# State-space B loaded in its final layout, and C turned with full 128x128 transposes, in a two-layer hybrid backbone step

## The chip, the cores and the metric

The kernel is one program on one NeuronCore of a Trainium2 chip. The time is device microseconds of one launch, the median of several runs. The engines are named as in the profile: PE is the matrix engine (PEld its weight loads), DVE the vector engine, ACT the scalar engine, POOL the general engine, SP the engine that issues most DMAs.

## What is computed

The reference is one inference step of a backbone with two layers over 128 context tokens and 512 latent tokens, 1024 channels wide. A layer normalises and shifts x, projects it once, runs three branches (a gated DeltaNet with scans in both directions, a diagonal complex state-space layer called S5, and a pooling mixer), adds the gated branches through an output projection and ends with a convolutional feed-forward network (FFN). What matters here is S5's input and output matrices: 32 groups, 64 complex states each, 16 channels.

```
bb_re = f_re[..., None] * b_re - f_im[..., None] * b_im      # b (G, P, 16), f (G, P)
bb_im = f_re[..., None] * b_im + f_im[..., None] * b_re
bu_re = einsum("blgc,gpc->blgp", u, bb_re)                   # u (B, L, G, 16)
x = scan of bu with the powers of lambda, once per direction
y = einsum("blgp,gcp->blgc", x_re, c_re) - einsum("blgp,gcp->blgc", x_im, c_im)
```

In DRAM `ssm_b_*[l]` is (32 groups, 64 states, 16 channels) and `ssm_c_*[l]` is (32 groups, 16 channels, 64 states), in float32.

## The kernel before

All activations lie channel-major: a tile is 128 channels by 640 tokens (512 latent, 128 context). A projection (`mm3`, lines 377 to 389) multiplies a 128-column tile of weights with eight such tiles; weights and activations are split into two float32r parts each, and three products per pair are added, so a tile of 1024 rows is 48 matmuls of 320 columns. The weights of a tile come by one 512 KB DMA on SP's queue (`wraw`, line 359, four buffers, shared with the modulation's weights `wada`, line 443), ACT makes the upper part (`whi`, line 371) and DVE the lower part (`wlo`, line 372), each in two halves with four buffers.

The S5 branch of a layer (`s5_chain`) is a chain of dependent steps: u is projected, sent to DRAM and read back in another order by eight SP loads (line 1044); `s5_params` makes the tables; `s5_in` (lines 909 to 930) turns the table of each quad of groups with four 128x128 transposes per part (line 915) and multiplies (line 920); `s5_scan` runs the recurrence on DVE; `s5_out` makes y. A `Weave` fills the chain's gaps: wherever the chain yields a number of microseconds, pieces of independent work (projections of the z gates, pools, branch gates, q and k, and parts of the modulation at line 446) are emitted for as long. Within these orders a scheduler with a simulated timeline sets the order of each engine's instructions; each engine then runs its own in order, and waits in order. SBUF space comes from an arena that hands out columns; a tile waits until the last users of its columns are done.

`s5_load` issues the parameter loads on POOL's queue: the rates and states (line 713), the step sizes (line 716), then B and C, real and imaginary, each as 32 rows (one per group) of 1024 values (lines 717 to 719). For layer 0 it is emitted at the start; for layer 1 it is one of the pieces that hang on the tiles of layer 0's FFN, with `s5_params` four pieces later, shortly before the last two tiles of the FFN and the next norm (`turn`, with its DVE lines 572 and 581).

`s5_params` first transposes the rates (line 735), has ACT and DVE make exponentials, sines and the powers of lambda (lines 749 to 829), and brings B and C to the layout [(direction, state), (group, channel)], 128 partitions by 512 columns: for each of the four tensors and each of the 16 channels a transpose of a [32 groups, 64 states] block (line 841) gives the upper 64 partitions of a PSUM bank and a product with the identity (line 842) the same in the lower 64, and ACT moves the bank to SBUF in the order of channels (line 845). Then DVE multiplies B with f (lines 862 to 867) and the skip weights are turned (line 876). The copies of ACT through PSUM carry line 235 in the profile, since a helper records them.

Of the kernel before, what the change touches and what calls it, by code (L numbers as in the profile page):

```python
# [17 lines left out]
P = 128  # L18
# [11 lines left out]
G = 32  # L30
# [10 lines left out]
WK, WB = 4, 4               # blocks of a split weight tile, and how many tiles stand  # L41
# [4 lines left out]
# columns of the constant table  # L46
C_ID, C_D16, C_TF, C_TB, C_BD = 0, 128, 144, 272, 400  # C_D16: row c' of a 32-row block against column c
C_M = 528                       # masks of the levels: the halves of 32 against each other, of 64; of a
                                # triangle in every second block, the other one in those between: 16, 32, 64
C_HALF = C_M + 5 * 128          # first and second half of 32  # L50
C_I16 = C_HALF + 2
C_EDGE = C_I16 + 16             # 4 windows x (8 left, 8 right)
C_POSR = C_EDGE + 64            # 4 tiles x 8 rows
C_POSC = C_POSR + 32            # 4 tiles x 64 columns
# [3 lines left out]
def constants():  # L58
# [26 lines left out]
    for n, w in enumerate(POOL_WINDOWS):  # L85
        h = w // 2
        for t in range(h):
            c[:, C_EDGE + 16 * n + t] = np.float32(w) / np.float32(t + h)
        for t in range(h - 1):          # t-th of the last h-1 positions
            c[:, C_EDGE + 16 * n + 8 + t] = np.float32(w) / np.float32(w - 1 - t)  # L90
# [4 lines left out]
class Arena:  # L95
    """SBUF in pages of some columns. A page holds data of one type at a time: a tile that stands while
    any of its columns is taken. Columns are handed out in program order, those free longest first,
    and next to blocks of the same size."""

    def __init__(self, pool, pages):  # L100
        self.pool = pool
        self.pages = [Page(i, n) for i, n in enumerate(pages)]
        self.clock = self.made = 0
        self.keep = True                # the largest page is kept free
        self.side = False               # of the work being emitted: a chain of steps, or what fills its gaps

    def take(self, cols, dt=F32, stays=False, most=None, big=False):
# [3 lines left out]
        for pg in self.pages:  # L111
# [3 lines left out]
            for s in pg.gaps(k):  # L115
# [4 lines left out]
                if stays:               # what stays long fills the pages already begun  # L120
                    key = (key[0], far, odd, not pg.blocks, key[-1])
# [18 lines left out]
class Page:  # L140
# [5 lines left out]
    def gaps(self, k):  # L146
        """Starts of the free places of k units: at either end of a gap, and every k units."""
        at = 0
        for b, e in self.blocks + [(self.n, self.n)]:
            if b - at >= k:  # L150
                yield from range(at, b - k + 1, k)
                yield b - k
            at = e
# [11 lines left out]
class Part:  # L165
    """Some columns of a Buf; the last part to go frees it."""
# [10 lines left out]
class Blocks:  # L177
    """Tiles of up to WK blocks, one after the other."""
# [10 lines left out]
class Weave:  # L189
    """Emits a chain of dependent steps with pieces of independent work in between: the chain yields  # L190
    how long (us of TensorE) it would leave the engine idle at a point."""
# [7 lines left out]
    def add(self, cost, fn, weights=None):  # L199
        """weights: prepares what fn takes, one piece of work ahead."""  # L200
# [23 lines left out]
class ScalarE:  # L224
    """The engine; remembers its last instructions that want another table set than that of Ln and Exp."""
# [15 lines left out]
def together(*gens):  # L241
    """Steps of several chains in turn."""
# [17 lines left out]
def hybrid_dit_kernel(ctx: ExitStack, tc: tile.TileContext, a, outs, depth=DEPTH, taps=None):  # L260
# [47 lines left out]
    def hv(ap):  # L308
        """[P, NT] as two halves."""
        return ap.rearrange("p (h n) -> p h n", h=2)  # L310

    # ------------------------------------------------------------------ parameters
    def rows_load(name, rows, E):
        """rows: list of (dram rows [r, 128], first row)."""
# [5 lines left out]
    def to_cols(name, rt, n):  # L320
        """The first n rows as columns [P, n]."""
# [9 lines left out]
    def load_params(l, E):  # L331
        fc = a["ffn_conv"][l].rearrange("t (r c) -> t r c", c=P)
        o = 0 if l else -56                                    # layer 0's b_ada and norm1_g come with glob
# [21 lines left out]
    # ------------------------------------------------------------------ weights  # L355
    def wraw(src, c0, nk, ncols):
        """Weight rows of src (nk*128, .) columns c0.. as [P, nk, ncols]."""
# [4 lines left out]
    def wsplit(raw, m):  # L362
        """128 columns of a raw block as two float32r parts whose sum is the block."""
# [13 lines left out]
    def mm3(ps, w, hs, first=True, last=True, M=P):  # L377
        """ps[M, 2, HF] (+)= w^T h with the products hi*hi, hi*lo and lo*hi."""
# [12 lines left out]
    def mm3k(ps, w, k, h_, first, last):  # L391
        """The part of mm3 of one tile of h; ps: the two halves."""
# [7 lines left out]
    def mmh(ps, w, k, h_, h, first, last):  # L400
        """The part of mm3 of one tile of h, one half."""
# [5 lines left out]
    def split(src, hi, lo, scale=None):  # L407
        """src [P, n] float32 (times scale, a power of two) -> float32r parts."""
# [13 lines left out]
    class Stream:  # L422
        """m-tiles of a weight matrix."""
# [7 lines left out]
    # ------------------------------------------------------------------ adaLN  # L431
    def ada_pieces(l, p, mod, grp, E=None):
        """Columns grp*2048.. of the modulation into mod [P, 2, 48], in pieces."""
# [18 lines left out]
        def finish():  # L452
# [5 lines left out]
            # column (j, b) of the group is m-tile grp*16 + 4*j + b  # L458
# [8 lines left out]
    # ------------------------------------------------------------------ norms  # L467
    @contextmanager
    def ln_exp():
        """ScalarE's table set that has both Ln and Exp, for what is emitted inside."""  # L470
# [8 lines left out]
    def rsq(ps2, n, scale, dst, bias=None):  # L479
        """dst = (scale*ps + eps)^-1/2 * e^bias over [P, NT] in two halves."""  # L480
# [9 lines left out]
    def square_sum(tot, x, i):  # L490
        """tot += x^2"""
# [8 lines left out]
    def spans(cut):  # L500
        """Columns and stream of the parts before and after a cut of the latents."""
        return ((0, cut, 0),), ((cut, LAT, 0), (CX, NT, 1))

    def last_tiles(xs, ws, hs, gate, cut, tot, sq, between, done):
        """The last two tiles (weights ws) of a projection onto x, all of them up to the cut first; between(): when
        the first is through; done(h): after each part. tot: the squares of the tiles before, then also of the last
        but one; sq: of the last."""
# [29 lines left out]
    def turn(xs, ws, hs, gate, tot, A, B, raws):  # L537
        """The last two tiles of a projection onto x, h = x / rms(x) * A + B per stream (A, B [P, 2, 8]; tot: the
        squares of the tiles before), and the first products of the next two weight tiles, as h comes; also an
        instruction that what follows on VectorE should queue behind."""  # L540
# [87 lines left out]
    def finale(xs, xg, ws, hs, gate, tot):  # L628
        """The last two tiles of the last projection, the norm, token-major again; xg: the tiles before times
        the norm's weights."""  # L630
# [43 lines left out]
    def scales(mod, c0, g):  # L674
        """(1 + scale) * g per stream."""
# [13 lines left out]
    def residual(x, ps, gate, i):  # L689
        """x += gate * ps per stream; gate [P, 2, 8]."""  # L690
# [6 lines left out]
    def conv3(y, r, w0, w2):  # L697
        """y (= w1*u) += w0*u[t-1] + w2*u[t+1] inside each stream."""
# [4 lines left out]
    # ------------------------------------------------------------------ S5  # L703
# [3 lines left out]
    def s5_load(l, E, kept):  # L707
# [9 lines left out]
        for nm in ("ssm_b_re", "ssm_b_im", "ssm_c_re", "ssm_c_im"):  # L717
            ld[nm] = ar.take(SP * GC)
            E.dma_start(ld[nm].f[:G, :], a[nm][l].rearrange("g x y -> g (x y)"))
# [8 lines left out]
    def s5_params(ld):  # L728
        """Discretisation; tables over [(dir, p), g]."""
# [23 lines left out]
        # sin and cos: ang - 2 pi round(ang / 2 pi), the multiple taken off in parts  # L753
# [14 lines left out]
        # cos(r) = sin(pi/2 - |r|)  # L768
# [4 lines left out]
        # powers 0..9 of lb over [ri, power, g]  # L773
# [7 lines left out]
        def cmul(dst, x, y, n):  # L781
            """dst[:, ri, n] = x * y (complex, all [P, 2, n, G])."""
# [11 lines left out]
        # f = (lb - 1) / lam  # L794
# [15 lines left out]
        # tables in the order each half (direction) wants: H = 0 forward, 1 backward  # L810
        cp = small("s5_cp", 2 * 10 * G)                        # C side: forward 0..9, backward 9..0
        q["cp"] = cp.rearrange("p (r j g) -> p r j g", r=2, j=10)
        bp = small("s5_bp", 2 * 8 * G)                         # B side: forward 7..0, backward 0..7
# [7 lines left out]
        # step of the recurrence over [ri, g]: lb^8 and its imaginary part signed  # L821
# [9 lines left out]
        # b and c transposed to [(dir, p), (g, channel)]  # L831
        tr = {}
        W = G * GC + GC
        kept, temp = ld["kept"], ar.take(3 * W)
        for nm in ("ssm_b_re", "ssm_b_im", "ssm_c_re", "ssm_c_im"):
            raw = ld[nm]
            ps = sm()
            for c in range(GC):
                src = (raw.f[:G].rearrange("g (p c) -> g c p", c=GC)[:, c] if "_b_" in nm
                       else raw.f[:G, c * SP:(c + 1) * SP])  # L840
                PE.transpose(ps[0:SP, c * G:(c + 1) * G], src, ident[:G, :G])
                PE.matmul(ps[SP:P, c * G:(c + 1) * G], src, ident[:G, :G], start=True, stop=True,
                          tile_position=(0, SP))
            t = Part((kept if "_c_" in nm else temp).f[:, W * (nm[-1] == "m"):][:, :W])
            S.activation(t.f[:, :G * GC].rearrange("p (g c) -> p c g", c=GC),
                         ps.rearrange("p (c g) -> p c g", c=GC), AF.Copy)
            raw.free()
            tr[nm] = t
        q["cre"], q["cim"] = tr["ssm_c_re"], tr["ssm_c_im"]
        bre, bim = tr["ssm_b_re"], tr["ssm_b_im"]  # L850
# [8 lines left out]
        t0 = Part(temp.f[:, 2 * W:2 * W + G * GC])  # L859
# [8 lines left out]
        temp.free()  # L868
# [1270 lines left out]
```

## Time and profile before

| | |
|---|---|
| median of three runs | 2631.55 us (2629.29 to 2636.67) |
| span of the profiled execution | 2633.5 us (of its time only the span is listed) |
| PE busy | 2501.0 us, 95% |
| DVE, ACT, POOL busy | 1592.6, 996.0, 543.3 us |
| mean granted TensorE clock | 0.966 |
| DMA | 296.29 MB, mean 113 GB/s |

The busy time of an engine is the time in which it runs an instruction. Engines run beside each other, so shares don't add up. The granted clock is the share of TensorE's full speed that the chip gave it: 1.00 is 2.4 GHz, 0.50 is 1.2 GHz. A wait is put down to the instruction whose end released it.

### The profile page before, as it was taken

The numbers are of one execution on the slowest core, as the hardware profiler recorded it, in microseconds if no ns is written. First come the engines' busy times: TensorE is split into PE (matmuls) and PEld (weight loads), VectorE is DVE, ScalarE is ACT, GpSimd is POOL, SyncE is SP. The second block draws the span as 40 slices with busy tenths as digits, with TensorE's granted clock in tenths as the row PEclk, the third lists the DMA queues.
The fourth block names the chain that finished last, engine by engine and source line by source line (L and its number), as shares of the span: only waits on it lengthen the run. The fifth ranks groups of instructions, "written<-read, shape, count | busy, mean of one in ns | idle before, by whom it ended". The sixth has DMA issues, their size and how long they took to land. (4 is left out here: it accounts for less than half of the span.)

```text
span 2633.5 us, 44415 instructions
## 1 busy us (share of the span) xinstructions
PE 2501.0 (95%) x17593; PEld 2366.6 (90%) x17593; DVE 1592.6 (60%) x3250; ACT 996.0 (38%) x1796; POOL 543.3 (21%) x552
## 2 busy tenths in 40 slices
PE   8989999998899999999988989999988999999998
PEld 6868988998899989999977979979888999999998
DVE  5467874269785543644565587733797866445355
ACT  4233343354234432433333423423532445334243
POOL 2241150134451000000123213301345420000000
PEclk9799999999899999999978989999999999999999
DMA  9642327434352355222227223374434422222221
GB/s 302 99 133 84 112 74 230 119 123 134 119 164 88 107 177 168 77 76 73 76 73 99 56 73 106 88 220 112 135 131 139 154 73 73 73 80 74 73 73 65
DMA packets 381635, 296.29 MB, mean 113 GB/s; under 512 B 33578, under 2 KB 336372, under 8 KB 381428
## 3 DMA queue, kind: packets, MB, share of 16 engines
q1 hardware_dynamic: 377892, 286.53, 38.0%
q0 software_dynamic: 3168, 6.68, 1.0%
q8 instruction: 139, 2.28, 0.4%
q14 instruction: 68, 0.56, 0.1%
q10 hardware_dynamic: 368, 0.25, 0.0%
HBM read 250.92 MB, written 42.48 MB: 111 GB/s over the span
## 5 line engine op out<-in xcount | busy, mean ns | idle before, releaser
L384 PE MATMUL acc<-pg,whi 128*128 128x320 f32 x4064 | 948.5, 314 | 7.6 <-ACT pg L235 5.5
L386 PE MATMUL acc<-pg,whi 128*128 128x320 f32 x4064 | 942.5, 312 | 3.1 <-DVE pg L411 3.0
L388 PE MATMUL acc<-pg,wlo 128*128 128x320 f32 x4064 | 936.4, 311 | 9.4 <-DVE wlo L372 9.4
L384 PEld LDWEIGHTS acc<-pg,whi 128*128 128x128 f32 x4064 | 683.3, 190 | 47.6 <-issue 22.3
L372 DVE TENSOR_TENSOR wlo<-wraw,whi 128x512 fp32r<-128x512 f32 (+1 forms) x538 | 406.2, 761 | 524.8 <-ACT whi L235 516.2
L388 PEld LDWEIGHTS acc<-pg,wlo 128*128 128x128 f32 x4064 | 686.4, 190 | 13.3 <-DVE wlo L372 9.6
L386 PEld LDWEIGHTS acc<-pg,whi 128*128 128x128 f32 x4064 | 687.4, 190 | 8.5 <-DVE pg L411 4.1
L235 ACT ACTIVATE whi<-wraw 128x512 fp32r<-128x512 f32 (+1 forms) x538 | 331.8, 623 | 926.9 <-PE acc L386 708.5
L235 ACT ACTIVATE pg<-pg 128x640 f32<-128x640 f32 (+8 forms) x335 | 223.3, 682 | 254.6 <-DVE pg L1993 56.6
L235 ACT ACTIVATE pg<-sm 128x512 f32<-128x512 f32 (+12 forms) x249 | 115.6, 486 | 274.3 <-PE sm L915 64.7
L235 ACT ACTIVATE pg<-acc 128x640 f32<-128x640 f32 (+3 forms) x196 | 126.7, 654 | 52.5 <-PE acc L388 35.2
L411 DVE TENSOR_TENSOR pg<-pg,pg 128x640 fp32r<-128x640 f32 x84 | 70.6, 847 | 41.1 <-ACT pg L235 36.0
L700 DVE SCALAR_TENSOR_TENSOR pg<-pg,cols_f 128x511 f32<-128x511 f32 x126 | 63.8, 548 | 42.3 <-ACT pg L235 42.2
L713 POOL DMA_DIRECT2D pg<-in_ssm_lambda_re_dram x2 | 1.2, 578 | 408.2 <-DVE pg L732 408.2
L691 DVE SCALAR_TENSOR_TENSOR pg<-acc,mod,pg 128x320 f32<-128x320 f32 x56 | 30.8, 550 | 77.1 <-PE acc L388 77.0
L1682 POOL TENSOR_TENSOR pg<-pg,pg 128x640 f32<-128x640 f32 x21 | 40.2, 1915 | 175.0 <-DVE pg L1680 110.8
L235 ACT ACTIVATE pg<-acc,cols_f 128x640 f32<-128x640 f32 (+1 forms) x88 | 68.3, 776 | 0.0
L1680 DVE SCALAR_TENSOR_TENSOR pg<-pg,acc 128x640 f32<-128x640 f32 x48 | 39.2, 816 | 42.8 <-PE acc L388 39.1
L701 DVE SCALAR_TENSOR_TENSOR pg<-pg,cols_h 128x511 f32<-128x511 f32 x126 | 63.5, 546 | 0.0
L569 POOL TENSOR_SCALAR pg<-pg,ada_a 128x320 f32<-128x320 f32 (+2 forms) x27 | 26.5, 990 | 158.1 <-DVE pg L691 102.9
L446 PE MATMUL sm<-wada,silu_c 128*32 128x512 f32 x320 | 55.2, 604 | 0.8 <-DMA wada<-in_w_ada_dram 0.8
L903 POOL TENSOR_TENSOR pg<-pg,pg 128x512 f32<-128x512 f32 (+1 forms) x32 | 53.8, 1684 | 1.6
(397 smaller groups left out, 3065.8 us busy)
## 6 DMA issues: line engine op xcount, KB each, us to landing
wraw<-in_w_in_dram SPq DMA_DIRECT2D x96, 512.0 KB, 4.4
wraw<-in_ffn_w_up_dram SPq DMA_DIRECT2D x88, 512.0 KB, 3.9
wada<-in_w_ada_dram SPq DMA_DIRECT2D x80, 512.0 KB, 4.5
wraw<-in_ffn_w_down_dram SPq DMA_DIRECT2D x32, 512.0 KB, 3.7
mg_dram<-pg SPq DMA_DIRECT2D x32, 320.0 KB, 2.2
pg<-mg_dram SPq DMA_DIRECT2D x32, 320.0 KB, 4.7
wraw<-in_w_out_dram SPq DMA_DIRECT2D x16, 512.0 KB, 3.8
pg<-in_w_ada_dram SPq DMA_DIRECT2D x6, 1024.0 KB, 12.1
```

The source lines that it names most:

```text
L235: ins = self.engine.activation(out, in_, func, **kw)
L372: V.tensor_sub(lo, src, hi)
L384: PE.matmul(ps[:M, h, :HF], hi[:, k, :M], hh[:, h * HF:(h + 1) * HF], start=first and k == 0, stop=False)
L386: PE.matmul(ps[:M, h, :HF], hi[:, k, :M], hl[:, h * HF:(h + 1) * HF], start=False, stop=False)
L388: PE.matmul(ps[:M, h, :HF], lo[:, k, :M], hh[:, h * HF:(h + 1) * HF], start=False, stop=last and k == n - 1)
L411: V.tensor_sub(lo.r, src, hi.r)
L446: PE.matmul(ps[q:q + 32, :], silu_c[:, k, :], t[:, j * 512:(j + 1) * 512], start=k == 0, stop=k == KT - 1, tile_position=(0, q))
L700: V.scalar_tensor_tensor(y[:, b + 1:e], r[:, b:e - 1], w0, y[:, b + 1:e], op0=OP.mult, op1=OP.add)
L701: V.scalar_tensor_tensor(y[:, b:e - 1], r[:, b + 1:e], w2, y[:, b:e - 1], op0=OP.mult, op1=OP.add)
L903: E.tensor_tensor(oo, oo, t.f, op=OP.add if r else OP.subtract)
L1680: V.scalar_tensor_tensor(hv(g_.f), hv(g_.f), 1.0, ps[:, :, :HF], op0=OP.add, op1=OP.mult)
L1682: GP.tensor_tensor(g_.f, g_.f, mg.f, op=OP.add)
```

## The change

`s5_load` now loads B straight into the layout in which it is used, into the first 64 partitions, in runs of 16 channels, and copies these to the other 64 partitions by a DMA that reads SBUF. C is loaded with (group, channel) on the partitions, four blocks of 128 rows side by side, and each row twice, once for each direction. In `s5_params` B needs no array operation any more; C is turned by four transposes of a [128, 128] block for the real and four for the imaginary part, and ACT moves each bank as it stands. The scratch tile of the products with f has its own space. All comments and docstrings of the file are dropped too, line by line, so that line numbers move little.

```
@@ s5_load @@
-        for nm in ("ssm_b_re", "ssm_b_im", "ssm_c_re", "ssm_c_im"):
-            ld[nm] = ar.take(SP * GC)
-            E.dma_start(ld[nm].f[:G, :], a[nm][l].rearrange("g x y -> g (x y)"))
+        with nc.allow_non_contiguous_dma(reason="runs of 16 channels"):
+            for nm in ("ssm_b_re", "ssm_b_im"):
+                ld[nm] = t = ar.take(G * GC)
+                E.dma_start(t.f[:SP].rearrange("p (g c) -> p g c", c=GC), a[nm][l].rearrange("g p c -> p g c"))
+                E.dma_start(t.f[SP:], t.f[:SP])
+        for nm in ("ssm_c_re", "ssm_c_im"):
+            ld[nm] = t = ar.take(4 * 2 * SP)
+            tv = t.f.rearrange("q (t d p) -> q t d p", t=4, d=2)
+            src = a[nm][l].rearrange("(t g) c p -> (g c) t p", t=4)
+            for d in range(2):
+                E.dma_start(tv[:, :, d], src)
@@ s5_params @@
-        tr = {}
         W = G * GC + GC
-        kept, temp = ld["kept"], ar.take(3 * W)
-        for nm in ("ssm_b_re", "ssm_b_im", "ssm_c_re", "ssm_c_im"):
-            raw = ld[nm]
+        kept, t0b = ld["kept"], ar.take(G * GC)
+        for n, nm in enumerate(("ssm_c_re", "ssm_c_im")):
             ps = sm()
-            for c in range(GC):
-                src = (raw.f[:G].rearrange("g (p c) -> g c p", c=GC)[:, c] if "_b_" in nm
-                       else raw.f[:G, c * SP:(c + 1) * SP])
-                PE.transpose(ps[0:SP, c * G:(c + 1) * G], src, ident[:G, :G])
-                PE.matmul(ps[SP:P, c * G:(c + 1) * G], src, ident[:G, :G], start=True, stop=True,
-                          tile_position=(0, SP))
-            t = Part((kept if "_c_" in nm else temp).f[:, W * (nm[-1] == "m"):][:, :W])
-            S.activation(t.f[:, :G * GC].rearrange("p (g c) -> p c g", c=GC),
-                         ps.rearrange("p (c g) -> p c g", c=GC), AF.Copy)
-            raw.free()
-            tr[nm] = t
-        q["cre"], q["cim"] = tr["ssm_c_re"], tr["ssm_c_im"]
-        bre, bim = tr["ssm_b_re"], tr["ssm_b_im"]
+            for t in range(4):
+                PE.transpose(ps[:, t * P:(t + 1) * P], ld[nm].f[:, t * P:(t + 1) * P], ident)
+            t = Part(kept.f[:, W * n:][:, :W])
+            S.activation(t.f[:, :G * GC], ps, AF.Copy)
+            ld[nm].free()
+            q["cre" if n == 0 else "cim"] = t
+        bre, bim = ld["ssm_b_re"], ld["ssm_b_im"]
...
-        t0 = Part(temp.f[:, 2 * W:2 * W + G * GC])
+        t0 = t0b
...
-        temp.free()
+        for t in (t0, bre, bim):
+            t.free()
```

## Rows read from the trace of the kernel before

**Rows 1.** The page, part 1: busy time, share, instructions of each engine.
```profile
PE 2501.0 (95%) x17593; PEld 2366.6 (90%) x17593; DVE 1592.6 (60%) x3250; ACT 996.0 (38%) x1796; POOL 543.3 (21%) x552
```

**Rows 2.** Stretches: length, busy of PE, PEld, DVE, ACT, POOL; granted clock, DMA.
```profile
71.00:105.50 34.50, 34.50 (x199) 26.71 (x198) 5.28 (x30) 5.98 (x12) 0.00 (x0) 0.56 0.86 75
105.50:131.00 25.50, 25.50 (x162) 23.24 (x161) 24.68 (x62) 6.17 (x8) 13.56 (x11) 0.92 0.36 117
131.00:145.00 14.00, 4.62 (x25) 2.85 (x25) 13.97 (x13) 0.70 (x1) 11.05 (x11) 0.70 0.03 3
1302.50:1337.00 34.50, 34.50 (x199) 26.76 (x198) 5.34 (x19) 6.17 (x10) 2.42 (x3) 0.57 0.12 39
1337.00:1360.00 23.00, 23.00 (x143) 22.98 (x144) 18.35 (x79) 9.69 (x15) 0.00 (x0) 0.90 0.31 83
1360.00:1400.00 40.00, 28.30 (x154) 25.42 (x153) 38.28 (x64) 16.40 (x35) 24.60 (x24) 0.87 0.37 107
```

**Rows 3.** Groups by line, PE, 71 to 105.5 us; busy, mean ns, idle.
```profile
L842 PE MATMUL sm<-cst,pg 32*64 32x32 f32 x128 | 26.7, 298 | 0.0
```

**Rows 4.** Timeline of PE, layer 0; start, duration, instruction.
```profile
71.30 0.22 PE L841 MATMUL sm<-cst,pg 32*64 32x32 f32 x1
...
105.44 0.27 PE L876 MATMUL sm<-cst,s_dr 8*128 8x8 f32 x1
105.64 0.90 PE L384 MATMUL acc<-pg,whi 128*128 128x320 f32 x2
...
109.48 0.45 PE L386 MATMUL acc<-pg,whi 128*128 128x320 f32 x2
109.77 0.46 PE L388 MATMUL acc<-pg,wlo 128*128 128x320 f32 x2
```

**Rows 5.** Timeline of PE, layer 1.
```profile
1302.80 0.22 PE L841 MATMUL sm<-cst,pg 32*64 32x32 f32 x1
...
1336.85 0.27 PE L876 MATMUL sm<-cst,s_dr 8*128 8x8 f32 x1
```

**Rows 6.** Timeline of PE, the first two groups of line 915.
```profile
144.33 1.06 PE L915 MATMUL sm<-cst,pg 128*128 128x128 f32 x4
...
151.25 0.60 PE L915 MATMUL sm<-cst,pg 128*128 128x128 f32 x4
```

**Rows 7.** Waits of ACT and DVE, 60 to 130 us; total, times, longest.
```profile
ACT pg L235 <- PE sm L842: 28.5, 4, 7.7
...
DVE s_dc L878 <- PE sm L876: 12.1, 1, 12.1
```

**Rows 8.** Waits of PE, 60 to 180 us.
```profile
PE acc L388 <- DVE wlo L372: 9.4, 1, 9.4
```

**Rows 9.** Waits of PE, 1260 to 1440 us.
```profile
PE acc L405 <- DVE pg L581: 8.2, 3, 4.2
```

**Rows 10.** Timeline of ACT, layer 0.
```profile
89.52 1.28 ACT L235 ACT_TABLE_LOAD   x1
```

**Rows 11.** Timeline of POOL: the first load of layer 0, the last of layer 1.
```profile
31.83 0.51 POOL L719 DMA_DIRECT2D pg<-in_ssm_b_re_dram  x1 [20.00 <-PE sm L1183]
...
1298.16 0.49 POOL L719 DMA_DIRECT2D pg<-in_ssm_c_re_dram  x1 [0.89 <-DVE pg L411]
```

**Rows 12.** DMA issues: queue, count, KB each, median us to landing.
```profile
pool_w<-in_pool_w_dram SPq DMA_DIRECT2D x8, 64.0 KB, 2.3
...
pg<-in_ssm_b_re_dram POOLq DMA_DIRECT2D x2, 128.0 KB, 4.5
...
wab<-in_w_in_dram SPq DMA_DIRECT2D x2, 64.0 KB, 2.3
...
s_ls<-in_ssm_log_step_dram POOLq DMA_DIRECT2D x2, 0.2 KB, 5.3
```

**Rows 13.** Timeline of SP, layer 0.
```profile
82.17 6.33 SPq L1044 DMA_DIRECT2D pg<-u_dram  x8
```

**Rows 14.** Timeline of DVE, layer 0.
```profile
71.74 0.68 DVE L372 TENSOR_TENSOR wlo<-wraw,whi 128x512 fp32r<-128x512 f32 x1
```

## The prediction

> **What bounds the kernel now.** I read the page's busy times first: TensorE (PE) is busy for 2501.0 of 2633.5 us [rows 1], so most of what is taken off PE comes off the time, unless PE then waits for something else. Next comes the table by stage [rows 2], which tells what PE is busy with in the two stretches where the state-space parameters of a layer are made, 71 to 105.5 us (layer 0) and 1302.5 to 1337 us (layer 1). PE is never idle there, but its granted clock is 0.56 and 0.57, and VectorE (DVE) does only 5.28 and 5.34 us of work in 34.5 us. The groups by line [rows 3] and the code show what PE does there: 64 transposes of line 841 and 64 products of line 842 (two passes each, hence x128) in turn, every one on a 32x64 corner of the array. The timelines [rows 4, 5] give the edges: line 841 begins at 71.30 and line 876, the first instruction behind the block, at 105.44; in layer 1 1302.80 and 1336.85. So the two blocks hold PE for 34.14 and 34.05 us, 68.2 together, and nothing else runs on PE meanwhile. The waits [rows 7] show who stands behind them: ScalarE (ACT) waited 28.5 us in four pieces for line 842, and behind these evictions in its queue stand the exponentials and sines of the parameters; DVE waited 12.1 us for line 876.
>
> **The blocks go.** All 256 array operations of both layers are taken out: 68.2 us of PE. Just behind the block the clock is still low: the seven pair-to-pair steps from 105.64 to 109.48 take 3.84 us, where a step at full clock is 0.29 us (109.48 to 109.77) [rows 4], so 7 x 0.29 = 2.0 would do. That is 1.8 us per layer that goes with the block, 3.6 in all, taken alike for layer 1. Gross 71.8 us.
>
> **The transposes that come.** Per layer two groups of four 128x128 transposes. Line 915 does just such a group: 0.60 us at full clock, 1.06 where the clock was low [rows 6]. I take the full clock, since dense products stand directly in front: 4 groups x 0.60 = 2.4 us; with the low clock it would be 4.2. Net 71.8 - 2.4 = 69.4 us. The Trainium skill, TensorE: Matmul & The Clock Gate, Part 4: PE-mode transpose, says that transposes do not count as activity for the clock as products do; the low clock in rows 2 agrees, and if eight transposes pulled the clock down again the gross would be smaller by the 3.6 us of the tail. The four evictions of the transposes replace eight of about 1 us on ACT and hang on no wait of PE.
>
> **The loads.** B came as 2 loads of 32 rows and C the same; now POOL issues per layer two loads of B with 2048 runs of 64 bytes, two copies of the lower half of B to the upper, and four loads of C with 512 runs of 256 bytes. An issue is 0.5 us on POOL [rows 11], so four more are 2 us on an engine with 21% busy [rows 1]: nothing. The new wait is that of each copy for the landing of its load, with POOL's later DMAs, C's among them, queued behind it; and PE waits for C. No row shows 2048 short runs from POOL. From below: 1024 runs of 64 bytes from SP landed in 2.3 us, as long as 64 KB in runs of 512 bytes [rows 12], so 2048 runs take 4.6 us, twice that, or the 4.5 us of today's 128 KB load. From above: 64 runs of 4 bytes from POOL landed in 5.3 us [rows 12]; if every run cost its share, 83 ns, a load would take 170 us. I take 7 us, near the row with the same run length, plus 4.5 for a copy. Two loads and copies one after the other and then C (4.5): 7 + 4.5 + 7 + 4.5 + 4.5 and 3 us of issues = 30.5 us. In layer 0 the first load was issued at 31.83 [rows 11], so C is there at 62, before PE comes to it at 71: no cost. In layer 1 the loads were held by SBUF space until 1298.16 [rows 11]; the new tiles are half as wide and should come earlier, and I take nothing, with 1298.2 + 7 + 4.5 + 1 + 4.5 - 1302.8 = 12.4 us as the upper end. The Trainium skill, DMA: Bandwidth & Descriptors, Specifications, speaks against this part: it wants at least 512 bytes per run for the full rate. At 64 KB rows 12 show no such price, 2.3 us with either run length; if the rate were halved, the loads would land 5 us later and layer 0 would still not wait.
>
> **What is late next.** The block covered for DVE. In layer 0 PE reaches the first transposes of the chunk inputs (line 915) at 144.33 [rows 6]. Between 105.64 and there it works 144.3 - 105.6 - 9.4 = 29.3 us, the 9.4 being a wait for DVE's weight part `wlo` [rows 8], and without the slow clock 27.5. After the change these pieces begin at 71.30 + 1.2 (transposes) + 0.2 = 72.7 and are done at 100.2. DVE, however, did 5.28 + 24.68 + 13.97 = 43.9 us in 71 to 145 [rows 2], all ahead of line 915 but 0.5 us. From 71.5, with 2 us for ACT's sines (a table load is 1.28 us [rows 10]) and no other hole, it is through at 116.9. PE then waits 16.7 us, 7.3 more than the 9.4 of today, either at `wlo` or at line 915. I take 7.3 us given back; from below 0 or a gain of the whole 9.4, if later pieces of the weave are put in front, and from above 16.7, if today's wait stays and the new one is added. In layer 1 DVE did 5.34 + 18.35 + 38.28 = 62.0 us between 1302.5 and 1400 [rows 2], while PE's stretch from 1337 to 1400 without 1.8 of slow clock and with 1.2 of transposes takes 62.4 us. DVE must then be full and still wait some 4 us for ACT's two table loads and four small functions: 4 us given back; today's wait of 8.2 us for DVE's line 581 [rows 9] is in these 62.4, so the ends are 8 gained and 8 lost. The chunk inputs themselves come back from DRAM by loads that SP issues from 82.17 to 88.5 [rows 13], before PE can want them at 100: nothing. The weights of the later woven pieces are queued on SP behind these and go out from 88.5; what they delay lies inside the wait for DVE until 116.9, as long as they land by about 105.
>
> **The sum.** 2633.5 - 69.4 + 7.3 + 4.0 = 2575.4 us for the profiled execution, of which only the span is listed. The span stands 2.0 us above the median of the runs, 2631.55, so I forecast 2573 us.
>
> **Rivals.** *All of it stays.* The weave's order is made anew around a shorter block, and pieces of independent work fill the holes of DVE. For it: PE had such pieces up to 144 us and was idle only 9.4 us. Against it: DVE is busy for 38.65 of the 39.5 us from 105.5 to 145 [rows 2]. Time 2633.5 - 69.4 - 2 = 2562. *DVE and C both late.* Today's wait in layer 0 stays and 16.7 us are added, layer 1 loses 4 and C comes 12.4 us late there: 33.1 given back, 2633.5 - 36.3 - 2 = 2595. *The block filled a hole.* PE could not have started the woven pieces before 105 anyway, and the time stays at 2632. Against it: line 384 starts directly behind the block with no idle time [rows 4], and DVE made the last part of its weights at 71.74 [rows 14]. *Slower:* the short runs cost POOL's queue a price per run. The place is the two B loads, which C waits behind; the point from which it decides is where C lands later than the block ended, 31.8 + 2x + 9 + 3 + 4.5 = 105.4, so x = 28.5 us per load or 14 ns per run. At twice that, 57 us, C lands at 162 and each layer loses 57 us: 2633.5 + 2 x 57 - 2 = 2746. For it only the 83 ns of the upper bound; against it the 2.2 ns per run of the 1024-run load [rows 12].
>
> **Chances.** My forecast 0.60 (its own range 2564 to 2588), all of it stays 0.20, both late 0.13, filled a hole 0.04, slower 0.03. About 0.3%, 8 us, is what a measurement can tell from no change. Faster is 0.60 + 0.20 + 0.13 = 0.93, the same 0.04, slower 0.03. The range reaches from rival one with today's 9.4 us wait gone too, 2553, to a little past rival two, 2600.
>
> **What would show it.** Right: PE's span of instructions from line 735 to line 876 is 1 to 2 us in each layer, or the pieces in between are products of the weave; no stretch of some 30 us at clock 0.5 is left near 71 and 1300; PE's busy time falls to about 2430; its waits for DVE (`wlo`, line 915, the lines around 581) grow by some 11 us. Wrong: PE waits for a DMA of C, POOL stands for tens of us in front of a B copy, or PE's waits for DVE grow by 30 us or more; or PE's busy time falls by 70 and the time by much less, in a stage that I did not look at, such as the recurrence, whose start moves.

## The result, and the profile after

The changed kernel takes 2590.12 us (median of 4 runs, 2585.26 to 2599.07) against 2630.72 us for the kernel before on the same chip: ratio 0.9845, 95% interval 0.9821 to 0.9869. The gain is 40.6 us, where 58 were forecast. The profiled spans differ by 43.3 us (2633.5 and 2590.2).

The page's busy times of the changed kernel answer to [rows 1]: PE does 60.3 us less, but the span shrinks by only 43.3, so PE's idle time grew by 17.0 us, from 132.5 to 149.5.

```profile
PE 2440.7 (94%) x17225; PEld 2321.6 (90%) x17225; DVE 1608.3 (62%) x3250; ACT 989.8 (38%) x1792; POOL 555.2 (21%) x560
```

The block itself went as forecast. The timeline of PE of the changed kernel in layer 0 (start, duration, instruction) answers to [rows 4] (line 745 was line 735, the new transposes are line 847; behind them lines stand 3 higher, so line 918 was 915): eight transposes in 1.09 us where 34 us had been, and the dense pairs behind them, from the second one on, at 0.46 us.

```profile
73.65 0.49 PE L745 MATMUL sm<-cst,pg 32*128 32x32 f32 x5
74.07 1.09 PE L847 MATMUL sm<-cst,pg 128*128 128x128 f32 x8
75.10 0.22 PE L879 MATMUL sm<-cst,s_dr 8*128 8x8 f32 x1
75.25 0.56 PE L384 MATMUL acc<-pg,whi 128*128 128x320 f32 x2
75.66 0.46 PE L386 MATMUL acc<-pg,whi 128*128 128x320 f32 x2
```

In layer 1 (answers to [rows 5]) the two groups stand between products of the projections, 0.65 and 0.60 us:

```profile
1305.14 0.65 PE L847 MATMUL sm<-cst,pg 128*128 128x128 f32 x4
...
1308.74 0.60 PE L847 MATMUL sm<-cst,pg 128*128 128x128 f32 x4
```

The loads from POOL's queue (count, KB each, median us to landing), to [rows 12]; PE never waited for one of them:

```profile
pg<-in_ssm_c_re_dram POOLq DMA_DIRECT2D x4, 128.0 KB, 5.6
...
pg<-pg POOLq DMA_DIRECT2D x4, 128.0 KB, 4.7
pg<-in_ssm_b_re_dram POOLq DMA_DIRECT2D x2, 128.0 KB, 6.1
```

Where the rest went shows only when the whole span is cut into stages at points of equal meaning: the end of the state-space branch, the first product of the turn behind the DeltaNet branch, the first transpose of the next layer's parameters. The table by stage (length, busy of PE, PEld, DVE, ACT, POOL, granted clock, DMA share, GB/s), first the kernel before, then the changed one; three rows are layer 0, three layer 1:

```profile
0.00:407.20 407.20, 372.53 (x2748) 335.78 (x2750) 270.53 (x655) 144.54 (x268) 124.27 (x160) 0.92 0.51 133
407.20:828.70 421.50, 396.41 (x2835) 371.82 (x2835) 270.80 (x489) 164.89 (x316) 136.40 (x111) 0.97 0.47 147
828.70:1302.50 473.80, 472.01 (x3197) 452.64 (x3196) 243.07 (x462) 180.06 (x297) 15.80 (x23) 1.00 0.35 104
1302.50:1704.90 402.40, 367.99 (x2629) 345.15 (x2629) 271.61 (x660) 144.63 (x277) 118.74 (x136) 0.92 0.36 83
1704.90:2133.70 428.80, 402.26 (x2863) 374.36 (x2863) 268.52 (x490) 165.36 (x317) 137.16 (x111) 0.98 0.47 145
2133.70:2633.50 499.80, 489.77 (x3334) 486.85 (x3332) 268.08 (x498) 196.47 (x323) 10.94 (x12) 1.00 0.24 70
```

```profile
0.00:381.20 381.20, 332.91 (x2498) 304.09 (x2499) 269.89 (x648) 136.45 (x259) 125.45 (x164) 0.94 0.54 139
381.20:830.00 448.80, 415.30 (x2897) 385.60 (x2896) 276.93 (x496) 169.68 (x322) 136.26 (x111) 0.95 0.45 142
830.00:1303.20 473.20, 471.10 (x3189) 451.48 (x3187) 242.36 (x460) 179.16 (x295) 20.75 (x26) 1.00 0.35 104
1303.20:1663.80 360.60, 335.01 (x2477) 323.34 (x2480) 276.25 (x660) 142.42 (x277) 123.40 (x136) 0.97 0.41 95
1663.80:2088.20 424.40, 393.89 (x2842) 367.53 (x2843) 274.06 (x490) 165.80 (x318) 138.15 (x111) 0.98 0.46 146
2088.20:2590.20 502.00, 492.52 (x3333) 489.54 (x3332) 268.81 (x498) 196.31 (x323) 11.18 (x12) 0.99 0.24 70
```

What to see (an idle time is a stage's length less PE's busy time): layer 1's parameters start at 1303.2 us instead of 1302.5. Layer 0 gained nothing; layer 1, 1331.0 us before and 1287.0 after, gained 44.0. In layer 0 the first stage is 26.0 us shorter, but idle time rose from 34.7 to 48.3 us, and 66 products fewer were done in it than the block's own 184 explain (x2748 to x2498; 192 passes went, 8 came). They are done in the next stage, whose count rises by 62. That stage, in which the change has no part, became 27.3 us longer: 12.6 us for the moved products, 8.4 us more idle time (25.1 to 33.5) and 6.3 us more slow clock (a clock of 0.95 instead of 0.97). Slow clock here is the part of PE's busy time that the withheld clock cost: busy time multiplied by one less the granted clock, summed over the clock's records.

Split in this way, each whole layer reads as follows (us, before and after; the work is busy time less slow clock):

| layer | work at full clock | slow clock | idle |
|---|---|---|---|
| 0 | 1202.9, 1184.0 | 38.0, 35.3 | 61.6, 83.9 |
| 1 | 1221.9, 1199.6 | 38.1, 21.8 | 71.0, 65.5 |

Both layers lost about the same work. In layer 0 nearly all of the slow clock came back and idle time rose by 22.3 us; in layer 1 neither happened. By the views of PE's waits, summed over layer 0 by the engine waited for, the waits for DVE grew from 30.2 to 35.7 us, those for ACT from 15.8 to 26.7 and those for DMA from 10.8 to 18.8; in layer 1 the waits for DVE fell from 36.6 to 32.4.

The three longest holes that follow the parameters in layer 0's first stage make 20 of its 48.3 us of idle time. PE's timeline in the changed kernel:

```profile
102.94 3.26 PE L446 MATMUL sm<-wada,silu_c 128*32 128x512 f32 x8 [3.90 <-DMA wada<-in_w_ada_dram]
...
117.91 0.90 PE L388 MATMUL acc<-pg,wlo 128*128 128x320 f32 x2 [8.04 <-DVE wlo L372]
118.61 0.73 PE L384 MATMUL acc<-pg,whi 128*128 128x320 f32 x2
...
123.01 0.60 PE L918 MATMUL sm<-cst,pg 128*128 128x128 f32 x4
...
330.84 0.69 PE L999 MATMUL sm<-pg,pg 128*81 128x128 f32 x2 [8.04 <-DMA hall_dram<-s_hall]
```

First a modulation weight lands late, then the weight part `wlo` is late, and 200 us later a product waits 8.04 us for a small matrix that goes through DRAM and back. In the kernel before, the longest wait of this last kind in layer 0 was 2.69 us (line 996 there):

```profile
367.81 0.42 PE L996 MATMUL sm<-pg,pg 128*81 128x128 f32 x2 [2.69 <-DMA pg<-hall_dram]
```

Behind the `wlo` hole the pairs take 0.73 us, not 0.46: a hole also costs clock. That `wlo` was late because of its place in DVE's queue, DVE's timeline and one row of POOL's show:

```profile
94.97 0.68 DVE L866 TENSOR_TENSOR pg<-pg,pg 128x512 f32<-128x512 f32 x1
...
97.70 4.62 DVE L901 TENSOR_TENSOR pg<-s_bp,pg 128x512 f32<-128x512 f32 x3
...
103.86 6.82 DVE L900 TENSOR_TENSOR pg<-s_bp,pg 128x512 f32<-128x512 f32 x5
...
116.28 3.27 DVE L372 TENSOR_TENSOR wlo<-wraw,whi 128x512 fp32r<-128x512 f32 x2
...
124.58 0.68 DVE L900 TENSOR_TENSOR pg<-s_bp,pg 128x512 f32<-128x512 f32 x1
```

```profile
95.73 7.55 POOL L900 TENSOR_TENSOR pg<-s_bp,pg 128x512 f32<-128x512 f32 x5 [0.69 <-DVE pg L866]
```

Both engines make chunk-input tables side by side, and DVE comes to `wlo` only at 116.28 us. In the stretch from 100 to 118 us DVE is busy for 17.96 of 18.00 us and PE for 6.58:

```profile
100.00:118.00 18.00, 6.58 (x21) 1.79 (x21) 17.96 (x15) 2.30 (x4) 17.37 (x15) 0.72 0.76 239
```

### The profile page after: what moved, and what is told of

Read it like the earlier page. It is cut to its first block, busy times and chain, and to the rows that moved or that the text cites. A ratio compares the mean times of both kernels' runs of the same rounds, so it can differ in the third digit from the quotient of the medians.

```text
span 2590.2 us, 43654 instructions
## 1 busy us (share of the span) xinstructions
PE 2440.7 (94%) x17225; PEld 2321.6 (90%) x17225; DVE 1608.3 (62%) x3250; ACT 989.8 (38%) x1792; POOL 555.2 (21%) x560
## 5 line engine op out<-in xcount | busy, mean ns | idle before, releaser
L372 DVE TENSOR_TENSOR wlo<-wraw,whi 128x512 fp32r<-128x512 f32 (+1 forms) x538 | 414.5, 776 | 524.3 <-ACT whi L235 518.1
L384 PEld LDWEIGHTS acc<-pg,whi 128*128 128x128 f32 x4064 | 681.4, 189 | 47.1 <-issue 16.7
L235 ACT ACTIVATE pg<-sm 128x512 f32<-128x512 f32 (+9 forms) x245 | 109.5, 470 | 207.1 <-PE sm L1502 59.4
L700 DVE SCALAR_TENSOR_TENSOR pg<-pg,cols_f 128x511 f32<-128x511 f32 (+1 forms) x130 | 65.9, 548 | 49.8 <-ACT pg L235 49.7
L411 DVE TENSOR_TENSOR pg<-pg,pg 128x640 fp32r<-128x640 f32 x84 | 68.6, 821 | 41.4 <-ACT pg L235 37.6
L701 DVE SCALAR_TENSOR_TENSOR pg<-pg,cols_h 128x511 f32<-128x511 f32 (+1 forms) x130 | 65.6, 546 | 0.0
L1683 DVE SCALAR_TENSOR_TENSOR pg<-pg,acc 128x640 f32<-128x640 f32 x48 | 39.0, 817 | 40.9 <-PE acc L388 35.3
L901 POOL TENSOR_TENSOR pg<-s_cp,pg 128x640 f32<-128x640 f32 x16 | 27.6, 1725 | 127.4 <-PE acc L388 55.8
## 6 DMA issues: line engine op xcount, KB each, us to landing
pg<-in_w_ada_dram SPq DMA_DIRECT2D x6, 1024.0 KB, 10.8
```

The source lines that it names most:

```text
L235: ins = self.engine.activation(out, in_, func, **kw)
L372: V.tensor_sub(lo, src, hi)
L384: PE.matmul(ps[:M, h, :HF], hi[:, k, :M], hh[:, h * HF:(h + 1) * HF], start=first and k == 0, stop=False)
L411: V.tensor_sub(lo.r, src, hi.r)
L700: V.scalar_tensor_tensor(y[:, b + 1:e], r[:, b:e - 1], w0, y[:, b + 1:e], op0=OP.mult, op1=OP.add)
L701: V.scalar_tensor_tensor(y[:, b:e - 1], r[:, b + 1:e], w2, y[:, b:e - 1], op0=OP.mult, op1=OP.add)
```

## The experiments

The first theory was that layer 1 keeps its block and layer 0 gives its own back to waits that the change brings; the rival, that each layer brings half. Two kernels do one layer alone, two others change the instructions' order or the place of one step.

**Layer 1 alone.**

```
NEW = ("", "bc")          # per layer: which of B and C go the new way
...
                if "b" not in NEW[l]:
                    ld[nm] = ar.take(SP * GC)
                    E.dma_start(ld[nm].f[:G, :], a[nm][l].rearrange("g x y -> g (x y)"))
                    continue
...                       # C, and the old and new ways in s5_params, likewise
```

> Layer 1 loads and turns B and C in the new way, layer 0 as before. Theory (layer 1 keeps its whole block, layer 0 gives its own back): in the two traces layer 1's stretch from its first projections to the end of its parameters went from 493.4 to 458.8 us, so this kernel should stand 35 to 43 us under the 2630.7 of the kernel before: 2588 to 2596, as fast as the changed kernel. Rival (each layer brings half of the 40.6 us): 2608 to 2613.

Measured: 2609.94 us, ratio 0.9918 (0.9889 to 0.9947). That is the rival's number, but not for its reason. Layer 0's counts are those of the kernel before (x2748, x3197) and it ends at 1299.7 us. Layer 1 takes 1305.3 us, 25.7 less than before, 18.3 more than in the changed kernel. Its rows:

```profile
0.00:403.50 403.50, 371.07 (x2748) 334.79 (x2749) 270.39 (x655) 144.72 (x268) 124.80 (x160) 0.92 0.51 134
...
825.90:1299.70 473.80, 471.99 (x3197) 452.66 (x3195) 243.21 (x461) 179.67 (x297) 20.62 (x28) 1.00 0.36 105
1299.70:1665.90 366.20, 333.57 (x2442) 319.70 (x2442) 272.71 (x660) 141.61 (x275) 120.08 (x136) 0.95 0.39 93
1665.90:2107.30 441.40, 411.22 (x2866) 381.12 (x2866) 268.10 (x490) 166.14 (x318) 139.30 (x109) 0.95 0.45 140
```

The state-space stage is within 6 us of the changed kernel's 360.6; the stage behind it takes 441.4 instead of 424.4 us, with the clock at 0.95 instead of 0.98.

**Layer 0 alone.**

```
NEW = ("bc", "")
```

> Layer 0 in the new way, layer 1 as before; up to the middle of layer 0's feed-forward part its instructions stand in the order of the changed kernel. Theory (layer 0 gives its block back): in the changed kernel's trace the first turn of the feed-forward part of layer 0 came at 830.0 us against 828.7 before, so the time is that of the kernel before within 8 us: 2623 to 2638. Rival (each layer brings half): 2608 to 2613. In the trace: the first chunk inputs near 123 us as in the changed kernel, the end of layer 0's blocks near 830.

Measured: 2654.1 us, ratio 1.0084 (1.0053 to 1.0115): slower than with no change at all, outside of both. Layer 0 ends at 1306.7 us, as the theory has it. But layer 1, the same work as before, takes 1348.5 us instead of 1331.0:

```profile
0.00:382.00 382.00, 332.88 (x2499) 302.52 (x2499) 269.68 (x648) 136.43 (x259) 124.42 (x164) 0.93 0.54 139
382.00:831.70 449.70, 414.72 (x2896) 385.63 (x2896) 277.42 (x496) 170.27 (x323) 137.28 (x111) 0.95 0.46 142
...
1306.70:1716.00 409.30, 374.38 (x2647) 350.14 (x2647) 273.63 (x660) 145.35 (x277) 117.41 (x136) 0.90 0.35 83
1716.00:2154.10 438.10, 402.13 (x2854) 376.48 (x2853) 272.89 (x490) 166.34 (x319) 137.09 (x111) 0.96 0.46 141
```

The two single layers add up to 1 us slower (-21.5 and +22.7), the two together are 40 faster. No fixed price per layer gives that.

**The kernel before in another order.**

```
-        kept, temp = ld["kept"], ar.take(3 * W)
+        kept, t0 = ld["kept"], ar.take(G * GC)
+        temp = ar.take(2 * W)
...
-        t0 = Part(temp.f[:, 2 * W:2 * W + G * GC])
```

> The kernel before with the same loads, transposes and products; only the scratch buffer t0 of the state-space parameters has a tile of its own in SBUF. The planner then puts the instructions of every engine in another order. This gives the size of what a new order alone moves. Theory (layer 0's gain was lost to waits that the change brings, not to the draw of the order): 2623 to 2638, within 0.3% of before. Rival (an order made anew is worth 10 to 20 us either way, and layer 0's loss is such a draw): outside of 2620 to 2641.

Measured: 2655.18 us, ratio 1.0087 (1.0061 to 1.0113). The theory's part on the order falls. The same instructions on the same data, with one scratch buffer elsewhere, cost 24 us. The scheduler then puts every engine's queue in another order; that the order costs it, and not the places in SBUF themselves, is argued, since no run parts the two. The profiled run was 5 us under the median. Its stages show where: the DeltaNet stage of layer 0 takes 431.0 us with the clock at 0.96 (before: 421.5, 0.97), layer 1's parts 408.1 and 433.5 (402.4 and 428.8).

```profile
0.00:400.50 400.50, 371.74 (x2764) 337.61 (x2768) 272.23 (x660) 144.25 (x269) 125.15 (x160) 0.92 0.51 135
400.50:831.50 431.00, 401.75 (x2818) 374.64 (x2818) 263.15 (x484) 164.11 (x314) 139.69 (x113) 0.96 0.47 145
831.50:1307.40 475.90, 472.79 (x3197) 452.53 (x3195) 243.00 (x461) 179.73 (x297) 15.40 (x20) 1.00 0.35 103
```

**The parameters first** (changed kernel).

```
+        q = qf()
         u = ar.take(4 * TS * NK)
...
-        q = qf()
         yield 12
```

> The changed kernel with the state-space parameters emitted ahead of the projections of u in both layers, so that the planner can put VectorE's chain (reduction, powers, factors, tables) earlier. Theory (VectorE and what stands in its queue set layer 0's first chunk inputs at 123 us): they come 5 to 15 us earlier, and 3 to 12 us of that reach the end: 2578 to 2587. Rival (SyncE's queue, in which the loads of U stand ahead of the weights of the woven pieces, sets it): no gain, 2587 to 2595.

Measured: 2584.52 us, ratio 0.9816 (0.9784 to 0.9847). The chunk inputs start at 108.6 us instead of 123.0, and layer 0 ends at 1286.2. The theory's ranges held. In the profiles layer 0 gained 17 us on the changed kernel's and layer 1, in another order, lost 11; layer 0's order is new as well.

The second theory, then: a new order moves each layer by some 10 us either way; apart from that, layer 1 keeps the block and layer 0 does not. Two kernels draw the order again, four work on layer 0's holes.

**The changed kernel in another order.**

```
-        kept, t0b = ld["kept"], ar.take(G * GC)
+        kept, t0b = ld["kept"], ar.take(3 * W)
```

> The changed kernel with the same work; only the scratch buffer t0 has a larger place in SBUF, so that the planner's order is drawn anew in both layers. Theory (the order's draw moves a kernel by 10 to 25 us, as the same edit moved the kernel before by 24, and the change itself is worth some 45 to 60): this kernel lies between 2580 and 2612, and what differs from the changed kernel lies in idle time and slow clock, in the DeltaNet stages for the most part, with PE's work at full clock within 8 us of the changed kernel's 2384. Rival (the changed kernel's order is no draw but what the mechanism gives): 2586 to 2594.

Measured: 2612.95 us, ratio 0.9932 (0.9912 to 0.9952), a microsecond above the theory's range and far outside the rival's. PE's busy time less its slow-clock part is 2387 us (the changed kernel: 2384). Layer 0 ends at 1310.4 us with 51.2 us idle in its first stage; layer 1 takes 1311.4, 24.5 more than the changed kernel's. So the theory held in that idle time and slow clock make the difference, but missed where: of the 31.6 us more, 27.6 lie in the two state-space stages (398.7 against 381.2, 370.7 against 360.6) and 4.9 in the DeltaNet stages (437.3 against 448.8, 440.8 against 424.4). The profiled run, 2623.57 us, was the slowest of eight and 10.6 above their median, so some of this is that one run.

```profile
0.00:398.70 398.70, 347.53 (x2570) 314.37 (x2572) 269.16 (x660) 141.21 (x267) 128.12 (x164) 0.94 0.52 139
398.70:836.00 437.30, 405.67 (x2826) 377.93 (x2827) 266.54 (x484) 163.71 (x315) 141.72 (x111) 0.95 0.45 141
...
1310.40:1681.10 370.70, 338.08 (x2487) 324.34 (x2490) 275.04 (x663) 142.82 (x277) 124.16 (x136) 0.95 0.39 93
1681.10:2121.90 440.80, 405.82 (x2824) 375.80 (x2824) 265.09 (x487) 164.46 (x316) 132.97 (x109) 0.95 0.44 139
```

**The kernel before, layer 1 in another order.**

```
-        kept, temp = ld["kept"], ar.take(3 * W)
+        kept, temp = ld["kept"], ar.take(4 * W)
```

> The kernel before with a larger scratch tile for the state-space parameters: the order of layer 0 stays, that of layer 1 is drawn anew. Theory (the kernel before has a lucky layer 1: 1331 us from its parameters to the end, where two other orders of the same work took 1341 and 1348): 2636 to 2656. Rival (1331 is what the order usually gives): 2625 to 2635.

Measured: 2635.54 us, ratio 1.0012 (0.9999 to 1.0026), on the border between both. Layer 1 takes 1333.8 us: this draw cost next to nothing.

**The loads of U from POOL** (changed kernel).

```
-            nc.sync.dma_start(U[t * GC:(t + 1) * GC], ...
+            GP.dma_start(U[t * GC:(t + 1) * GC], ...
```

> The changed kernel with the eight loads of U issued by POOL instead of SyncE; the order of the instructions is else almost that of the changed kernel. Theory (the weights of layer 0's woven pieces land late because SyncE issues the loads of U from 84.5 to 92.1 us ahead of them): PE's holes between 99 and 118 us, 3.9 us for a modulation weight and 8.0 us for wlo, shrink by 4 to 8 us, the first chunk inputs come near 117 instead of 123: 2582 to 2587. Rival (VectorE's parameters and tables alone set these holes): the holes stay, 2588 to 2595.

Measured: 2595.22 us, ratio 0.987 (0.984 to 0.99): no gain, as the rival had it, though not for its reason. PE's holes between 99 and 118 us went from 3.90 + 8.04 to 0.73 + 4.36 + 2.65 us, 4.2 us less, as the theory said, but the chunk inputs came at 125.9, not earlier:

```profile
99.81 1.05 PE L446 MATMUL sm<-wada,silu_c 128*32 128x512 f32 x4 [0.73 <-DMA wada<-in_w_ada_dram]
105.22 0.90 PE L384 MATMUL acc<-pg,whi 128*128 128x320 f32 x2 [4.36 <-ACT whi L235]
111.16 0.90 PE L388 MATMUL acc<-pg,wlo 128*128 128x320 f32 x2 [2.65 <-DVE wlo L372]
```

**Both, parameters first and U from POOL.** Its diff is the two above.

> Both edits of layer 0 together: the parameters ahead of the projections of u, and U's loads issued by POOL. Theory that the two holes are separate (VectorE's chain, SyncE's queue): 3 to 6 us under the kernel with the parameters first, 2578 to 2582. Rival (with VectorE early nothing waits for SyncE's queue): 2582 to 2588.

Measured: 2597.69 us, ratio 0.9876 (0.9848 to 0.9904), worse than either theory. PE stood 10.95 us for a modulation weight at 138.86, and POOL issued the loads of U only at 120.1 us, behind the products of the tables in its own queue.

**Two quads' tables wholly on POOL** (changed kernel).

```
-        for r, E in ((0, GP), (1, V)):
+        for r, E in ((0, GP), (1, GP if qd < 2 and not conj else V)):
```

> The changed kernel with the imaginary tables of the first two quads of chunk inputs made by POOL instead of VectorE (both layers). Theory (VectorE's queue sets layer 0's hole: the weight part wlo, which PE waited 8.0 us for, stood behind twelve table products of 1.5 to 1.75 us): six of these leave VectorE, the wait for wlo shrinks to 0 to 3 us, the recurrence of layer 0 starts 3 to 9 us earlier than 194.1: end 2580 to 2588, with a draw of the order of up to 10 us on top. Rival (the weights' loads set it, the 3.9 us for the modulation weight being part of the same lateness): the wait moves to ScalarE's or SyncE's part of the weight, the recurrence starts within 2 us of 194.1, 2587 to 2596.

Measured: 2589.01 us, ratio 0.9828 (0.9796 to 0.9859). The theory was right on the wait and the rival on the outcome: the wait for `wlo` is 0.80 us, the recurrence starts on PE at 194.0 (in the changed kernel at 194.1), and a new hole stands further on. POOL is busy for all of 95 to 125 us.

```profile
100.81 3.16 PE L446 MATMUL sm<-wada,silu_c 128*32 128x512 f32 x8 [4.36 <-DMA wada<-in_w_ada_dram]
...
106.22 0.56 PE L388 MATMUL acc<-pg,wlo 128*128 128x320 f32 x2 [0.80 <-DVE wlo L372]
...
136.19 1.92 PE L446 MATMUL sm<-wada,silu_c 128*32 128x512 f32 x4 [3.70 <-DMA wada<-in_w_ada_dram]
```

**Parameters first and the tables on POOL.** Again two diffs from above.

> Parameters first, and the same two quads of tables on POOL. Theory (VectorE was already early with the parameters first, and POOL then is the longer one): no gain over the kernel with the parameters first alone, 2580 to 2592. Rival (VectorE's queue still holds PE up): 2572 to 2580.

Measured: 2587.0 us, ratio 0.9832 (0.9811 to 0.9853): no gain, as the theory had it.

**Parameters first again, beside the changed kernel.** Nothing new is edited.

> The kernel with the parameters first once more, beside the changed kernel on the same chip, since 5.6 us were less than the spread of the single runs. Theory (VectorE's chain held layer 0 up; layer 0's half 17 us shorter, another draw of layer 1's half 11 us longer): 2581 to 2588, 3 to 9 us under the changed kernel. Rival (the difference was chance): within 3 us of the changed kernel.

> The changed kernel itself, on the chip of these runs, to compare with: 2587 to 2594.

Measured on one chip: 2583.17 us, ratio 0.9816 (0.9799 to 0.9834), and 2592.36 us, ratio 0.9850 (0.9835 to 0.9866). Parameters first is the fastest kernel of the study, 9 us under the changed one; the two intervals only just part. Its layer 0 ends at 1277.7 us, 25.5 earlier than the changed kernel's beside it, and its layer 1 takes 15.4 longer (17 and 11 were expected; layer 0 ended at 1286.2 in the run above, so one profile of a half is good to some 8 us):

```profile
0.00:375.00 375.00, 337.26 (x2556) 306.75 (x2560) 269.93 (x657) 139.88 (x266) 129.64 (x164) 0.96 0.55 147
375.00:800.70 425.70, 393.19 (x2841) 370.19 (x2839) 271.49 (x487) 163.69 (x317) 141.11 (x113) 0.97 0.47 145
```

## Why the prediction was half right

Time of each layer in the profiled execution, cut at the first transpose of layer 1's parameters, in us. Commas part the runs of one order, semicolons the orders. The kernels with U or tables on POOL are left out, since their orders are close to the one they come from and their layer 1 is within 6 us of it. Each value comes from one profiled run: where its time is on record it lies within 5 us of its kernel's median, but for the changed kernel with other places, 10.6 above.

| layer | block as before | the new way |
|---|---|---|
| 0 | 1302.5, 1299.7, 1296.3 (order of before); 1307.4 (other places) | 1303.2, 1306.7, 1303.2 (order of after); 1310.4 (other places); 1286.2, 1277.7 (parameters first) |
| 1 | 1331.0; 1333.8; 1348.5; 1341.0 | 1287.0, 1286.9 (order of after); 1305.3; 1311.4; 1298.1, 1302.3 (parameters first) |

Taking the mean of each order first, layer 0 takes 1303.5 us with the block and 1307.4 without it, parameters first left aside: nothing gained in either of the two new orders. With parameters first, whose edit aims at layer 0, as a third order the mean is 1298.9, a gain of 4.6. Layer 1 takes 1338.6 and 1301.0: 37.6 gained, with a spread of 8 to 10 us between orders on either side, so a standard error of some 6.5.

Step by step:

- *The blocks go, eight transposes come, 69.4 us net.* Right as PE's own work: 1.09 and 1.25 us stand where 34 did, each time at full clock. PE's busy time fell by 60.3, not 69.4. Summed over the clock's records, slow clock took 76.1 us of the busy time before and 57.1 after, 19.0 less, where the two blocks alone had held some 30 (68.2 x 0.44): 11 came back as slow clock elsewhere, some of it behind holes as at 117.91.
- *The loads cost nothing.* Right: 6.1 us for B (7 taken), 4.7 for the copy (4.5), 5.6 for C (4.5), and no wait of PE for them. Two parts were off at no cost: one issue of a B load held POOL for 1.12 us, not 0.5, and in layer 1 the last load of C was issued at 1302.16, 4.0 us later than in [rows 11], not earlier; PE came to it at 1308.74. The rule of the Trainium skill, DMA: Bandwidth & Descriptors, Specifications, that runs under 512 bytes miss the full rate, is not refuted, but small here: B in 64-byte runs takes 1.6 us more to land than the 4.5 us of [rows 12].
- *Layer 1 gives 4.0 us back.* Wrong in size, within what an order is worth: 44.0 gained in the kernel's own order, 37.6 in the mean of four, against 34.7 - 4.0 = 30.7. The 4.0 us were to be waits for DVE, but PE's waits for DVE in layer 1 fell by 4.2. Both kernels had a good draw here: the changed one stands 18.6 us under the mean of the other three new orders (1305.6), the one before 10.1 under that of its other three (1341.1).
- *Layer 0 gives 7.3 us back.* This is the step that failed: it gave back all 34.7. Its first half held, but for 6 us. The chunk inputs were to move from 144.33 to 116.9 and came at 123.01, 21.3 us earlier, with 11.9 us of named waits where 16.7 were allowed, and the recurrence started 26.0 us earlier (220.1 to 194.1). The unsaid second half did not hold: that what follows would simply move along, with no wait but those for DVE. By the end of the state-space branch 26.0 us were gained, 10 to 13 of them by putting off 66 products (66 x 0.15, or the 12.6 us of work that the next stage took over), while the wait for the matrix from DRAM grew from 2.69 to 8.04 us; and the DeltaNet stage, 27.3 us longer, took all of it. Over the whole layer the waits for DVE grew by 5.5 us, near the 7.3 forecast. What the forecast put at nothing was the rest: 10.9 us more waiting for ACT, 8.0 more for DMA, and 12 of the block's 15 us of slow clock, which came back elsewhere.

The forecast counted 27.4 + 30.7 = 58.1 us; the profiles show -0.7 + 44.0 = 43.3. So 28.1 too many in layer 0 are partly offset by 13.3 too few in layer 1: the right direction, and a time inside the range in part by luck. In the other order of the same change, 2612.95 us, the time would have lain outside it (2553 to 2600). The prediction had named this as a way to be wrong, a stage not looked at whose start moves.

Shown: layer 0's added idle time is not the draw of one order. The four profiles whose layer 0 has the block (two orders) have 58 to 62 us of idle time there, the six without it and without parameters first (two orders, and two close to them) 76 to 88. Also shown: part of the block can be had in layer 0, which ends at 1277.7 to 1287.5 us in three of the four runs with parameters first, some 20 of the 34.7 us; the fourth, 1303.9, is the one with U late. Argued, not shown: that the earlier start of DVE's chain is the cause, since these runs share nearly one order of layer 0, and a good draw would look the same. The `wlo` hole does not set layer 0's time: with tables on POOL it was gone, and the next late weight made a hole instead.

Open: which dependence in the DeltaNet stage turns the changed start into waits, and how much of its 27.3 us is the draw. That stage took from 418 to 451 us in layer 0 over all kernels (put-off products included), and 9.5 us longer in the kernel before by a new order alone. Open too is whether parameters first would keep its lead in other orders.

## What to carry to other kernels

Where a scheduler orders everything anew, a single before-and-after pair carries the draw of the order: run both versions in one or two other harmless orders before giving an edit its size. An edit that frees TensorE is worth its length only if the work behind it has its inputs; follow the feeding engine's queue to the next join, and the count of deferred work through the stage after. Cut both profiles at points of equal meaning and compare idle time, clock and instruction count of each stage.

## What the runs showed of the hardware

A DVE product of a chunk-input table, 128x512 float32, took 0.68 us at 124.58, when POOL did nothing, and 1.54 us (4.62 / 3) at 97.70, while POOL did the same kind of products at 1.51 us each (7.55 / 5). The weight part `wlo` took 0.68 us in [rows 14], with POOL idle, and 1.64 (3.27 / 2) at 116.28 beside POOL. The Trainium skill, SBUF — State Buffer, Terms, says that DVE and GpSimd take turns on one shared port pair, each holding it for a whole instruction; the trace agrees, the DVE product being 2.3 times as long. By an estimate from these rows DVE alone needs 1.36 us for two products and the two engines side by side 1.54, so sharing a table between them bought nothing. Moving six products from one to the other changed the time by no more than the runs spread (2589.01 and 2592.36 us).

In the changed kernel the clock fell behind PE's holes, not behind the new transposes: behind the eight full transposes pairs ran at 0.46 us, behind the 8.04 us hole at 0.73. A hole is not the only way to a low clock: in the block of the kernel before it was 0.56 with PE never idle [rows 2]. Whether the transposes or the small products made it fall there, no run parts; the prediction took rows 2 as a sign for the transposes.
